# Loading the value product's repeated weight block with its other six tiles, and preparing the fourth pair's right block one product sooner

## The chip, the cores and the metric

The kernel runs on one core of a Trainium2 chip. The metric is the device time of one execution in microseconds (us). The engines are TensorE (PE; its weight loads are listed as PEld), VectorE (DVE), ScalarE (ACT), GpSimd (POOL) and SyncE (SP), which here issues all DMAs.

## The reference

One layer of a streaming encoder, with 1024 positions of width 1024, in fp32. Two attentions run side by side, of 8 heads of 64 each: one over a band of 9 chunks of 64 positions with a learned bias, and one of the stick-breaking kind.

```python
def reference(x, w_in, b_gate, rel_bias, w_proj_a, w_proj_b, w_out,
              ln1_g, ln1_b, w_ffn_in, w_ffn_out, ln2_g, ln2_b):
    ...
        h = x @ w_in[l]
        qa, ka, va, qb, kb, vb, ga, gb = jnp.split(h, split_pts, axis=-1)
        ...
        y_a = chunk_band_attention(heads_a(qa), heads_a(ka), heads_a(va), rel_bias[l]) @ w_proj_a[l]
        y_b = stick_breaking_attention(heads_b(qb), heads_b(kb), heads_b(vb)) @ w_proj_b[l]
        gate_a = jax.nn.sigmoid(ga + b_gate[l, :D])
        gate_b = jax.nn.sigmoid(gb + b_gate[l, D:])
        mix = (gate_a * y_a + gate_b * y_b) @ w_out[l]
        x = layer_norm(DEEPNORM_ALPHA * x + mix, ln1_g[l], ln1_b[l])
        gu = x @ w_ffn_in[l]
        g, u = jnp.split(gu, 2, axis=-1)
        ffn = (jax.nn.silu(g) * u) @ w_ffn_out[l]
        x = layer_norm(DEEPNORM_ALPHA * x + ffn, ln2_g[l], ln2_b[l])
    return x
```

The change lies in the first product, `x @ w_in`.

## The kernel before

**How a product is made.** Every operand is split into a high part (rounded, by a cast on ScalarE) and a low part (what is left, by a subtraction on VectorE); the helper `split` does both, at lines 110 and 111. Each product of two operands is three matmuls: high by high, high by low, low by high. On top of that the kernel multiplies block matrices of 2 x 2 blocks with seven products instead of eight. The seven are called p1 to p7 and run in the order 1, 2, 6, 5, 7, 3, 4. Some of them need sums or differences of blocks as their weights, and VectorE makes those: for a pair called `p3`, `tap3` and `tbp3` are such differences (lines 151, 152, 153 and 159, of the raw left block `wLp3` and right block `wRp3`). `wbp3h` and `wbp3l` are the high and low part of `tbp3`, `wap3h` and `wap3l` those of `tap3`, and `wcp3` holds both parts for p3.

**The order of the work.** `work` is a list: four pairs of q and k columns (tiles p0 to p3), the fifth q and k pair (p4), then the value columns V of all heads (at index `V_AT`, 5), then the other q and k pairs, then the gates. `run_pairs` emits the seven steps of each in turn. The left block of a pair (`left`, line 129) and its right block (`right`, which calls `prep_right` at line 140 and `prep_last` at line 162) are emitted between the steps of the pairs ahead. For the first three lists of steps, p1 and p2 are emitted ahead of everything (`first=3`). At the end of each pair, line 388 (ScalarE) and line 389 (VectorE) scale and split q and k, and lines 335 and 336 store them (`q_dr`, `k_dr`).

**The value product.** Here the weights are the moving operand's blocks, and its accumulators are four banks (`v1_0` to `v1_3` for p1, used again by p6; `v2_0` to `v2_3` for p2). `v_load` asks for six raw tiles, the halves of blocks 0, 2 and 3 of V's weights: `wv0_0`, `wv0_1`, `wv2_0`, ... . `v_prepare` makes the operands of one product from them. Block 1 is needed in differences for p6 (lines 434, 435 and 436) and for p7 (line 438), and is loaded for each of them at line 432, as `wv1_60` and `wv1_61` for p6. The differences are written over the tiles that they read. The high and low parts are `vh6_0`, `vl6_0` (first half), `vh6_1`, `vl6_1`. Line 479 issues the matmuls, line 489 (ScalarE) and 491 (VectorE) take the results out of the banks into tiles `vc11_0` and so on, and line 459 stores them to `v_dr`.

**Who decides the order.** The program order above is where each instruction is written. A scheduler then places the instructions of each engine, except a few that are kept as written. Buffers come from rotating pools with fixed numbers (`gt` 3, `kp` 4, `op` 8): a new tile waits until the last reader of the tile that had its buffer is done. `cycle(QKV, ...)` takes buffers in turn from four pools that the attention uses later. SyncE issues all DMAs in one queue, in order.

Of the kernel before, what the change touches and what calls it, by code (L numbers as in the profile page):

```python
# [48 lines left out]
def hybrid_trunk_kernel(ctx: ExitStack, tc, x, xt, w_first, w_v, w_in, b_gate, rel_bias, w_proj,  # L49
# [14 lines left out]
    def slot(tag, name, dtype=F32):  # L64
        return pool.tile([P, 1024], dtype, tag=tag, name=name, bufs=SLOTS[tag])
# [3 lines left out]
    def cycle(tags, name, dtype=F32):  # L69

        turn_of[tags] = turn_of.get(tags, -1) + 1
        return slot(tags[turn_of[tags] % len(tags)], name, dtype)

    QKV = ("qs", "kh", "kl", "v")
# [9 lines left out]
    dma = nc.sync.dma_start  # L84
# [24 lines left out]
    def split(dst_h, dst_l, src):  # L109
        return (nc.scalar.copy(dst_h, src),  # L110
                nc.vector.tensor_tensor(dst_l, src, dst_h.bitcast(F32), ALU.subtract))  # L111
# [28 lines left out]
    def prep_right(W, nm, src, tag, tag_a=None):  # L140
        W["R"] = slot("gt", f"wR{nm}")
        dma(W["R"], src)
        right_sums_b(W, nm, tag)
        right_sums_a(W, nm, tag_a or tag)
# [17 lines left out]
    def prep_last(W, nm, tag):  # L162

        c = slot(tag, f"wc{nm}", F32R)
        split(c[:, LO], c[:, HI], W["R"][:, HI])
        W["c"] = c
# [69 lines left out]
    V_AT = 5  # L236
# [6 lines left out]
    def left(i):  # L243
        prep_left(Wa[i], f"p{i}", w_in[work[i][2]])

    def right(i):
        prep_right(Wa[i], f"p{i}", w_in[work[i][3]], "op")
        prep_last(Wa[i], f"p{i}", "kp")
# [161 lines left out]
    v_src = [[None] * 2 for _ in range(3)]  # L410
    v_ops = {}

    def v_load():

        for n, (blk, tags) in enumerate(((0, ("gt", "gt")), (3, ("gt", "kp")), (2, ("kp", "kp")))):
            for h, tag in enumerate(tags):
                v_src[n][h] = slot(tag, f"wv{blk}_{h}")
        for n, blk in ((0, 0), (2, 2), (1, 3)):
            for h in range(2):
                dma(v_src[n][h], w_v[blk, h])  # L420

    def v_prepare(p):

        put, sub = nc.vector.tensor_tensor, ALU.subtract
        v_ops[p] = []
        for h in range(2):
            X, U, Z = (v_src[n][h] for n in range(3))
            hi, lo = (slot("op", f"v{s}{p}_{h}", F32R) for s in "hl")
            src = {1: X, 2: Z, 5: X, 3: U, 4: Z}.get(p)
            if src is None:  # L430
                src = cycle(QKV, f"wv1_{p}{h}") if p == 6 else slot("gt", f"wv1_{p}{h}")
                dma(src, w_v[1, h])
                if p == 6:
                    put(X, src, X, sub)
                    put(src, U, X, sub)
                    put(Z, Z, src, sub)
                else:
                    put(src, U, src, sub)
            split(hi, lo, src)
            v_ops[p].append((hi, lo))  # L440

    def v_steps():
# [18 lines left out]
        def step(p, following):  # L461
# [3 lines left out]
            def run():  # L465
                if following:
                    v_prepare(following)
                if first:
                    for j in range(4):
                        tag = ("mm", "mm", "sc", "sc")[j] if accs is by else ("tr", "tr", "tr", "pv")[j]  # L470
                        accs[j] = bank(tag, f"v{p}_{j}")
                for h in range(2):
                    for j in range(4):
                        for i in range(2):
                            kt = 2 * h + i
                            xh_, xl_ = (x[:, j * P:(j + 1) * P] for x in ops_x[p][kt])
                            wh, wl = (w[:, (LO, HI)[i]] for w in v_ops[p][h])
                            for n, (a, b) in enumerate(((xh_, wh), (xh_, wl), (xl_, wh))):
                                mm(accs[j], a, b, start=(first and kt == n == 0),  # L479
                                   stop=(kt == 3 and n == 2), skip_group_check=True)  # L480
                for j in range(4):
                    acc = spread(accs[j])
                    if p == 4:
                        done("21", j, acc)
                        continue
                    name = {1: "11", 2: "11", 6: "12", 3: "12", 5: "22", 7: "22"}[p]
                    raw = tile_of(name, j)[1]
                    if p in (1, 6, 5):
                        nc.scalar.copy(raw, acc)
                    else:  # L490
                        nc.vector.tensor_tensor(raw, acc, raw, ALU.add)
                        done(name, j, raw)
# [9 lines left out]
            store_proj(i - len(work) + 9)  # L502

    def run_pairs(steps, left, right, also=lambda i: None, first=2, aside=lambda i: None,
                  then=lambda: None, wide=None):

        n = len(steps)
        for j in range(first):
            steps[j][0]()
            steps[j][1]()  # L510
        then()
        for i in range(n):
            rest = steps[i][2:] if i < first else steps[i]
            for j, p in enumerate(rest):
                p()
                if i == wide:
                    if j == 5:
                        left(i + 1)
                    if j == 6:
                        right(i + 1)  # L520
                        left(i + 2)
                    continue
                if j == 0 and i + 1 < n:
                    right(i + 1)
                if j == 1 and i + 2 < n and wide not in (i + 1, i + 2):
                    left(i + 2)
                aside(i)
            also(i)
# [74 lines left out]
    def left_again(i):  # L603
        Wa[i]["L"] = slot("gt", f"wLp{i}")
        dma(Wa[i]["L"], w_in[work[i][2]])
# [21 lines left out]
    def right_or_v(i):  # L627
        if i + 1 == V_AT:
            v_load()
            v_prepare(1)  # L630
        else:
            right(i + 1)

    run_pairs([v_steps() if i == V_AT else project(i) for i in range(1, len(work))],
              lambda i: left(i + 1) if i > 2 else left_again(3) if i == 2 else None,
              right_or_v, first=3, then=rest_of_start, also=aside_work, wide=V_AT - 1)
    first_gate = 2 * N_GATE
    first_w = begin_gate(first_gate, nc.vector)()

# [611 lines left out]
    def second_half():  # L1251
# [3 lines left out]
    plain_half(LO, ops_1[1] + ops_1[2], second_half)  # L1255
    prep_last(Wf[1], "f1", "op")
    run_pairs([up_steps(f) for f in range(1, NF)], lambda i: left_f(i + 1) if i > 1 else None,
              lambda i: right_f(i + 1), first=2, aside=next_piece, then=plain_rest)

# [3 lines left out]
    def load_plain(f0, f1, tags):  # L1263
        hs = []
        take = lambda name, dtype: cycle(tags, name, dtype)
        for f in range(f0, f1):
            hs.append(load_w(h_dr[f], f"h{f}", of("gt"), take, nc.vector) +
                      load_w(w_ffn_out[f * P:(f + 1) * P, :], f"fo{f}", of("gt"), take,
                             nc.vector))
        return hs  # L1270
# [88 lines left out]
    first = load_plain(0, 2, ("bw", "bw", "kp", "kp", "bw", "bw", "bw", "kp"))  # L1359
# [67 lines left out]
```

## Time and profile before

| what | value |
|---|---|
| runs | 1443.1, 1443.45, 1443.83 us (median 1443.45) |
| profiled execution | 1444.35 us, span 1442.6 us |
| PE busy | 1421.1 us (99%), 6696 matmuls |
| VectorE, ScalarE, GpSimd busy | 1028.6, 673.0, 267.8 us |
| granted TensorE clock | 0.994 mean |

The profile is of one execution. Its rows give a start in us from the start of the span, then a duration, the engine, the line of the kernel, the operation and the tiles (buffer numbers left out), the shape, and how many were merged (x12). In square brackets stands the idle time of the engine before the row and what ended it. A granted clock of 1.00 is TensorE at full speed.

### The profile page before, as it was taken

How to read it: one execution, taken by the hardware profiler on the slowest of the kernel's cores; microseconds unless marked ns; L12 is line 12 of the kernel's file. 1: busy time of each engine (PE TensorE's matmuls, PEld its weight loads, DVE VectorE, ACT ScalarE, POOL GpSimd, SP SyncE). 2: the span in 40 equal slices, each digit the busy share in tenths (PEclk: the TensorE clock that was granted, in tenths of full speed). 3: DMA queues.
4: the chain of work that ended last, by engine and by line, in shares of the span. 5: the costliest groups of instructions: out<-in, count | busy, mean ns of one | idle time of the engine just before them, and what ended most of it. 6: DMA issues, size and time to landing. Idle time of an engine off the chain costs nothing.

```text
span 1442.6 us, 19078 instructions
## 1 busy us (share of the span) xinstructions
PE 1421.1 (99%) x6696; PEld 1178.6 (82%) x6696; DVE 1028.6 (71%) x1638; ACT 673.0 (47%) x1171; POOL 267.8 (19%) x317
## 2 busy tenths in 40 slices
PE   9997999999999999999999999999999999999997
PEld 7785888888888888888888888888888888888886
DVE  8856565654777878887858966676777755978757
ACT  6443444555787888773313634444444433221201
POOL 0000000001555778850014000000000000100016
PEclk9998999999999999999999999999999999999999
DMA  7565357868677587867512123434444457786602
GB/s 248 149 203 165 127 205 220 283 205 251 195 214 193 166 239 239 270 197 274 178 37 95 55 106 127 143 143 157 161 160 146 150 201 260 287 306 240 204 15 103
DMA packets 102544, 263.99 MB, mean 183 GB/s; under 512 B 11040, under 2 KB 27424, under 8 KB 102448
## 3 DMA queue, kind: packets, MB, share of 16 engines
q1 hardware_dynamic: 102448, 262.77, 55.5%
q8 instruction: 53, 0.87, 0.3%
q14 instruction: 43, 0.35, 0.1%
HBM read 170.94 MB, written 88.11 MB: 180 GB/s over the span
## 4 chain that ended last, share of the span: by engine, by line
PE 93%; DVE 3%; ACT 1%; DMA 1%; issue 1%; POOL 0%; SPq 0%; POOLq 0%; DVEq 0%; ACTq 0%
PE sxf L180 16%; PE sxp L180 8%; PE szf L180 8%; PE dx L1350 6%; PE v L479 5%; PE gps L573 4%; PE szp L180 4%; PE syf L180 4%; PE dz L1350 3%; PE yAps L870 3%; PE syp L180 2%; PE tp_b L781 2%; PE tp_a L781 2%; PE ops L118 2%; PE ops L117 2%; PE ops L120 2%
## 5 line engine op out<-in xcount | busy, mean ns | idle before, releaser
L1306 POOL TENSOR_TENSOR wdyt<-wdyt 128x512 f32<-128x512 f32 x8 | 11.1, 1394 | 512.3 <-ACT h L1178 422.6
L758 POOL TENSOR_TENSOR w_b<-w_b,kp_b 128x511 f32<-128x511 f32 (+3 forms) x96 | 96.4, 1015 | 31.8 <-DVE kp_b L753 22.5
L753 DVE TENSOR_TENSOR_SCAN kp_b<-kp_b,ident_ps 128x512 f32<-128x512 f32 (+2 forms) x64 | 56.6, 885 | 23.3 <-ACT kp_b L750 22.4
L750 ACT ACTIVATE kp_b<-sc_b 128x512 f32<-128x512 f32 (+3 forms) x96 | 48.4, 504 | 30.7 <-PE sc_b L670 25.4
L1058 POOL TENSOR_TENSOR mv<-mv,neghalf 128x1 f32<-128x1 f32 x16 | 23.9, 1494 | 207.6 <-DVE mv L1057 207.6
L693 POOL MEMSET bias<- 64x64 f32 x2 | 0.3, 145 | 327.3 <-ACT bias L689 327.3
L180 PE MATMUL szf<-x1S63h,wcf 128*128 128x512 f32 x168 | 55.1, 389 | 0.0
L111 DVE TENSOR_TENSOR pt_b<-tp_b,pt_b 128x512 fp32r<-128x512 f32 (+1 forms) x96 | 50.0, 544 | 6.8 <-ACT pt_b L110 6.2
L1281 DVE TENSOR_TENSOR x<-dx,x 128x512 f32<-128x512 f32 x64 | 43.5, 687 | 14.9 <-PE dx L1350 14.9
L723 POOL TENSOR_SCALAR w_a<-w_a,st_a 128x640 f32<-128x640 f32 (+2 forms) x64 | 42.4, 667 | 61.6 <-PE sc_a L670 26.5
L111 DVE TENSOR_TENSOR sl<-h,sl 128x512 fp32r<-128x512 f32 x56 | 38.5, 687 | 20.1 <-ACT sl L110 20.1
L110 ACT CAST sl<-h 128x512 fp32r<-128x512 f32 x56 | 34.7, 619 | 36.2 <-PE syf L180 17.1
L110 ACT CAST pt_b<-tp_b 128x512 fp32r<-128x512 f32 (+1 forms) x96 | 47.5, 505 | 8.0 <-PE tp_b L781 7.6
L718 ACT ACTIVATE w_a<-w_a,st_a 128x640 f32<-128x640 f32 (+2 forms) x64 | 44.8, 700 | 12.4 <-DVE st_a L712 11.2
L118 PE MATMUL ops<-wl_o,mh 128*128 128x512 f32 x128 | 50.1, 392 | 0.0
L120 PE MATMUL ops<-wh_o,ml 128*128 128x512 f32 x128 | 49.9, 390 | 0.0
L117 PE MATMUL ops<-wh_o,mh 128*128 128x512 f32 x128 | 49.7, 391 | 0.0
L1178 ACT ACTIVATE h<-sxf 128x512 f32<-128x512 f32 x21 | 12.6, 598 | 77.7 <-PE sxf L180 77.7
L751 ACT ACTIVATE w_b<-sc_b 128x511 f32<-128x511 f32 (+3 forms) x96 | 48.6, 506 | 0.0
L781 PE MATMUL tp_b<-ident,w_b 128*128 128x128 f32 x288 | 47.8, 273 | 0.4 <-DVE pt_b L111 0.3
L111 DVE TENSOR_TENSOR pt_a<-tp_a,pt_a 128x512 fp32r<-128x512 f32 (+1 forms) x96 | 44.8, 485 | 4.6 <-ACT pt_a L110 3.1
L110 ACT CAST pt_a<-tp_a 128x512 fp32r<-128x512 f32 (+1 forms) x96 | 39.1, 432 | 11.0 <-PE tp_a L781 10.7
(1740 smaller groups left out, 4784.8 us busy)
## 6 DMA issues: line engine op xcount, KB each, us to landing
s_dr<-sl SPq DMA_DIRECT2D x112, 256.0 KB, 2.3
sd<-s_dr SPq DMA_DIRECT2D x56, 512.0 KB, 4.8
wLf<-in_w_ffn_in_dram SPq DMA_DIRECT2D x22, 512.0 KB, 4.5
wRf<-in_w_ffn_in_dram SPq DMA_DIRECT2D x22, 512.0 KB, 3.5
v_dr<-vc SPq DMA_DIRECT2D x16, 512.0 KB, 3.0
kh<-k_dr SPq DMA_DIRECT2D x32, 256.0 KB, 5.8
kl<-k_dr SPq DMA_DIRECT2D x32, 256.0 KB, 6.0
qs<-q_dr SPq DMA_DIRECT2D x16, 512.0 KB, 5.5
```

Of the source, the lines that this page charges most:

```text
L110: return (nc.scalar.copy(dst_h, src), nc.vector.tensor_tensor(dst_l, src, dst_h.bitcast(F32), ALU.subtract))
L111: nc.vector.tensor_tensor(dst_l, src, dst_h.bitcast(F32), ALU.subtract))
L117: mm(acc, lh, rh, start=(i == 0), stop=False)
L118: mm(acc, lh, rl, start=False, stop=False)
L120: mm(acc, ll, rh, start=False, stop=(i == n))
L180: mm(acc, lw[:, ks], rx, start=(first and kt == i == 0), stop=(kt == 3 and i == 2), skip_group_check=not first)
L479: mm(accs[j], a, b, start=(first and kt == n == 0), stop=(kt == 3 and n == 2), skip_group_check=True)
L573: mm(acc[hf], lw[:, ks], rx[k][:, (LO, HI)[hf]], start=(k == j == 0), stop=(k == KT - 1 and j == 2))
L753: nc.vector.tensor_tensor_scan(kp[:, 0:e], kp[:, 0:e], ident_ps()[:, 0:e], 0.0, ALU.mult, ALU.add)
L758: nc.gpsimd.tensor_tensor(be[:, m0:e], be[:, m0:e], kp[:, m0 - 1:e - 1], ALU.mult)
L781: tr(tp[:, (qb - lo_q) * P:(qb - lo_q + 1) * P], wt[qb - q0][:, (kb - qb) * P:(kb - qb + 1) * P], ident)
L1350: mm(acc, a, b, start=(first and i == n == 0), stop=(i == n - 1 == 1), skip_group_check=not first)
```

## The change

`v_load` takes two more buffers, `wv1_60` from the pool `kp` and `wv1_61` from the cycle, and loads block 1 into them directly after the other six tiles. `v_prepare` for p6 uses these tiles and loads nothing; for p7 it loads as before. `run_pairs` has a new argument, `then_right=2`: the right block of the fourth pair (p3) is emitted after p7 of the second pair (p1), and no longer after p6 of the third (p2). In between lay p3 and p4 of the second pair and p6 of the third. The call of `run_pairs` for the FFN does not pass the argument.

```diff
--- before.py
+++ after.py
@@ -415,26 +415,30 @@
         for n, (blk, tags) in enumerate(((0, ("gt", "gt")), (3, ("gt", "kp")), (2, ("kp", "kp")))):
             for h, tag in enumerate(tags):
                 v_src[n][h] = slot(tag, f"wv{blk}_{h}")
+        again = [slot("kp", "wv1_60"), cycle(QKV, "wv1_61")]
         for n, blk in ((0, 0), (2, 2), (1, 3)):
             for h in range(2):
                 dma(v_src[n][h], w_v[blk, h])
+        for h in range(2):
+            dma(again[h], w_v[1, h])
+        v_src.append(again)
 
     def v_prepare(p):
 
         put, sub = nc.vector.tensor_tensor, ALU.subtract
         v_ops[p] = []
         for h in range(2):
-            X, U, Z = (v_src[n][h] for n in range(3))
+            X, U, Z, Y = (v_src[n][h] for n in range(4))
             hi, lo = (slot("op", f"v{s}{p}_{h}", F32R) for s in "hl")
             src = {1: X, 2: Z, 5: X, 3: U, 4: Z}.get(p)
             if src is None:
-                src = cycle(QKV, f"wv1_{p}{h}") if p == 6 else slot("gt", f"wv1_{p}{h}")
-                dma(src, w_v[1, h])
+                src = Y if p == 6 else slot("gt", f"wv1_{p}{h}")
                 if p == 6:
                     put(X, src, X, sub)
                     put(src, U, X, sub)
                     put(Z, Z, src, sub)
                 else:
+                    dma(src, w_v[1, h])
                     put(src, U, src, sub)
             split(hi, lo, src)
             v_ops[p].append((hi, lo))
@@ -502,7 +506,7 @@
             store_proj(i - len(work) + 9)
 
     def run_pairs(steps, left, right, also=lambda i: None, first=2, aside=lambda i: None,
-                  then=lambda: None, wide=None):
+                  then=lambda: None, wide=None, then_right=None):
 
         n = len(steps)
         for j in range(first):
@@ -520,8 +524,10 @@
                         right(i + 1)
                         left(i + 2)
                     continue
-                if j == 0 and i + 1 < n:
+                if j == 0 and i + 1 < n and i + 1 != then_right:
                     right(i + 1)
+                if j == 2 and i + 2 == then_right:
+                    right(i + 2)
                 if j == 1 and i + 2 < n and wide not in (i + 1, i + 2):
                     left(i + 2)
                 aside(i)
@@ -633,7 +639,7 @@
 
     run_pairs([v_steps() if i == V_AT else project(i) for i in range(1, len(work))],
               lambda i: left(i + 1) if i > 2 else left_again(3) if i == 2 else None,
-              right_or_v, first=3, then=rest_of_start, also=aside_work, wide=V_AT - 1)
+              right_or_v, first=3, then=rest_of_start, also=aside_work, wide=V_AT - 1, then_right=2)
     first_gate = 2 * N_GATE
     first_w = begin_gate(first_gate, nc.vector)()
```

The number of instructions of each engine stays the same; their order changes from the second pair to the value product, and at the start of the attention. Lines of the changed kernel after 418 are shifted: 434, 435, 436 are now 437, 438, 439, line 459 is 463, and line 491 is 495.

The first place is VectorE (DVE), behind the low parts of the third pair's right block (the right block of p3 is `wRp3`, its left block `wLp3`; `c1_1` and `c2_1` are q and k of the second pair). Before:

```order
L195 TENSOR_TENSOR c2_1_643<-szp1_664,c2_1_643 128x512
L151 TENSOR_TENSOR tap3_749<-wRp3_747,wLp3_678 128x512
L159 TENSOR_TENSOR tap3_749<-wRp3_747 128x512
L152 TENSOR_TENSOR tbp3_750<-wRp3_747,tap3_749 128x512
L389 SCALAR_TENSOR_TENSOR c2_1_643<-c2_1_643,hi2_1_706 128x1024
L389 SCALAR_TENSOR_TENSOR c1_1_533<-c1_1_533,hi1_1_726 128x1024
L153 TENSOR_TENSOR tbp3_750<-wLp3_678,tbp3_750 128x512
L111 TENSOR_TENSOR wcp3_763<-wRp3_747,wcp3_763 128x512
L111 TENSOR_TENSOR wbp3l_755<-tbp3_750,wbp3h_754 128x1024
L111 TENSOR_TENSOR wap3l_760<-tap3_749,wap3h_759 128x1024
```

The same stretch of VectorE now:

```order
L151 TENSOR_TENSOR tap3_695<-wRp3_693,wLp3_678 128x512
L159 TENSOR_TENSOR tap3_695<-wRp3_693 128x512
L152 TENSOR_TENSOR tbp3_696<-wRp3_693,tap3_695 128x512
L195 TENSOR_TENSOR c2_1_643<-szp1_664,c2_1_643 128x512
L153 TENSOR_TENSOR tbp3_696<-wLp3_678,tbp3_696 128x512
L111 TENSOR_TENSOR wcp3_709<-wRp3_693,wcp3_709 128x512
L389 SCALAR_TENSOR_TENSOR c1_1_533<-c1_1_533,hi1_1_745 128x1024
L111 TENSOR_TENSOR wbp3l_701<-tbp3_696,wbp3h_700 128x1024
L111 TENSOR_TENSOR wap3l_706<-tap3_695,wap3h_705 128x1024
L389 SCALAR_TENSOR_TENSOR c2_1_643<-c2_1_643,hi2_1_725 128x1024
```

The three subtractions (lines 151, 152, 153) and line 159 now stand ahead of both steps of line 389, and that of `c2_1` comes last.

The second place is SyncE around V's weights (`rel_dr` is the table of the bias, `k_dr4` and `q_dr4` are k and q of the fifth pair). Before, the stretch that ends with the two loads of line 432 (the six loads lie further up):

```order
L335 DMA q_dr4_81<-hi1_4_1069 64x1024
L336 DMA q_dr4_81<-c1_4_959 64x1024
L335 DMA q_dr4_81<-hi1_4_1069 64x1024
L336 DMA q_dr4_81<-c1_4_959 64x1024
L432 DMA wv1_61_1155<-in_w_v_dram 128x1024
L459 DMA v_dr0_93<-vc11_0_1136 128x1024
L432 DMA wv1_60_1146<-in_w_v_dram 128x1024
```

The stretch of SyncE with these two loads (now line 423) now:

```order
L329 DMA rel_dr_213<-rel_sb_939 8x896
L421 DMA wv3_0_963<-in_w_v_dram 128x1024
L421 DMA wv3_1_964<-in_w_v_dram 128x1024
L423 DMA wv1_60_967<-in_w_v_dram 128x1024
L423 DMA wv1_61_968<-in_w_v_dram 128x1024
L335 DMA k_dr4_89<-hi2_4_1053 64x1024
L336 DMA k_dr4_89<-c2_4_1011 64x1024
L335 DMA k_dr4_89<-hi2_4_1053 64x1024
L336 DMA k_dr4_89<-c2_4_1011 64x1024
```

Before, `wv1_61` and `wv1_60` were issued behind the stores of the fifth pair's q, one of them behind the first store of V; now both stand ahead of the fifth pair's k as well.

The third place is VectorE in the value product (`c1_4` is q of the fifth pair, `v2_0` a bank of V's p2). Before:

```order
L389 SCALAR_TENSOR_TENSOR c1_4_959<-c1_4_959,hi1_4_1069 128x1024
L491 TENSOR_TENSOR vc11_0_1136<-v2_0_1162,vc11_0_1136 128x8x64
L491 TENSOR_TENSOR vc11_1_1138<-v2_1_1163,vc11_1_1138 128x8x64
L111 TENSOR_TENSOR vc11_0_1136<-vc11_0_1136 128x8x64
L491 TENSOR_TENSOR vc11_2_1140<-v2_2_1164,vc11_2_1140 128x8x64
L111 TENSOR_TENSOR vc11_1_1138<-vc11_1_1138 128x8x64
L491 TENSOR_TENSOR vc11_3_1142<-v2_3_1165,vc11_3_1142 128x8x64
L111 TENSOR_TENSOR vc11_2_1140<-vc11_2_1140 128x8x64
L111 TENSOR_TENSOR vc11_3_1142<-vc11_3_1142 128x8x64
L434 TENSOR_TENSOR wv0_1_962<-wv1_61_1155,wv0_1_962 128x1024
L435 TENSOR_TENSOR wv1_61_1155<-wv3_1_964,wv0_1_962 128x1024
L436 TENSOR_TENSOR wv2_1_966<-wv2_1_966,wv1_61_1155 128x1024
```

VectorE behind the same line 389 now:

```order
L389 SCALAR_TENSOR_TENSOR c1_4_959<-c1_4_959,hi1_4_1073 128x1024
L437 TENSOR_TENSOR wv0_0_961<-wv1_60_967,wv0_0_961 128x1024
L438 TENSOR_TENSOR wv1_60_967<-wv3_0_963,wv0_0_961 128x1024
L437 TENSOR_TENSOR wv0_1_962<-wv1_61_968,wv0_1_962 128x1024
L439 TENSOR_TENSOR wv2_0_965<-wv2_0_965,wv1_60_967 128x1024
L111 TENSOR_TENSOR vl6_0_1149<-wv1_60_967,vh6_0_1148 128x1024
L438 TENSOR_TENSOR wv1_61_968<-wv3_1_964,wv0_1_962 128x1024
L495 TENSOR_TENSOR vc11_0_1140<-v2_0_1162,vc11_0_1140 128x8x64
L439 TENSOR_TENSOR wv2_1_966<-wv2_1_966,wv1_61_968 128x1024
L111 TENSOR_TENSOR vl6_1_1156<-wv1_61_968,vh6_1_1155 128x1024
L111 TENSOR_TENSOR vc11_0_1140<-vc11_0_1140 128x8x64
L495 TENSOR_TENSOR vc11_1_1142<-v2_1_1163,vc11_1_1142 128x8x64
```

The differences of p6 (434 to 436 before, 437 to 439 now) come directly behind line 389, and the results of p2 are taken out of their banks between and behind them.

## The prediction

> **What bounds the kernel now.** I read the page first, for the share of each engine.
>
> ```profile
> span 1442.6 us, 19078 instructions
> PE 1421.1 (99%) x6696; PEld 1178.6 (82%) x6696; DVE 1028.6 (71%) x1638; ACT 673.0 (47%) x1171; POOL 267.8 (19%) x317
> ```
>
> PE is the bound nearly everywhere. The diff leaves the number of matmuls alone, so it can gain only what PE waits, or runs slowly, in the stretch it touches. Next came the waits of PE (engine, line, what it waited for; total us, times, longest).
>
> ```profile
> PE v L479 <- ACT vh L110: 9.3, 1, 9.3
> ...
> PE sxp L180 <- ACT wbp3h L110: 0.4, 1, 0.4
> ```
>
> One long wait stands out: a product of V (line 479) waits for `vh`, the high part of its weights. A short one names `wbp3h`, the fourth pair's right block (its tile p3). Those are the two things that the diff prepares differently. Third, the timeline of PE at the short one, and the steady pace from a run of 12 matmuls without a wait.
>
> ```profile
> 63.31 0.39 PE L180 MATMUL szp<-s13h,wap2l 128*128 128x512 f32 x1
> 64.11 0.50 PE L180 MATMUL sxp<-s24h,wbp3h 128*128 128x512 f32 x1 [0.41 <-ACT wbp3h L110]
> ...
> 65.70 0.39 PE L180 MATMUL sxp<-s24h,wbp3h 128*128 128x512 f32 x1
> 341.70 2.72 PE szp L180 x12
> ```
>
> The last row, a piece of the chain of waits, gives 2.72 / 12 = 0.227 us a matmul. From 63.31 to 65.70 are five steps (counted in the timeline): 2.39 us where 5 x 0.227 = 1.13 would do. **Stall A is 1.26 us**, not the 0.41 that the one wait shows. Fourth, the same for the long wait, and the windows around it (columns: window and length, busy of PE, PEld, DVE, ACT, POOL, then granted clock, DMA share, GB/s).
>
> ```profile
> 127.71 0.39 PE L479 MATMUL v<-vh,xl 128*128 128x512 f32 x1
> 137.38 1.65 PE L479 MATMUL v<-vh,s24h 128*128 128x512 f32 x3 [9.28 <-ACT vh L110]
> ...
> 143.66 0.39 PE L479 MATMUL v<-vh,s24h 128*128 128x512 f32 x1
> 127.70:137.40 9.70, 0.42 (x3) 0.02 (x1) 9.41 (x10) 2.15 (x4) 0.00 (x0) 0.77 0.77 264
> 137.40:143.20 5.80, 5.80 (x14) 4.34 (x15) 4.65 (x5) 2.77 (x3) 0.00 (x0) 0.50 0.21 56
> ```
>
> PE stands from 127.71 + 0.23 = 127.94 to 137.38, 9.44 us, and comes back at a granted clock of 0.50, which lasts 5.80 us. The matmul at 143.66 is the 16th after that at 127.71 (counted in the timeline): 15.95 us where 16 x 0.227 = 3.63 would do. **Stall B is 12.32 us**: 9.44 of waiting and 2.88 of slow clock.
>
> **Why stall A is there, and what the change does to it.** VectorE and ScalarE in front of it:
>
> ```profile
> 57.61 0.69 DVE L195 TENSOR_TENSOR c<-szp,c 128x512 f32<-128x512 f32 x1
> 58.21 0.69 DVE L151 TENSOR_TENSOR tap<-wRp,wLp 128x512 f32<-128x512 f32 x1
> ...
> 60.01 2.36 DVE L389 SCALAR_TENSOR_TENSOR c<-c,hi 128x1024 f32<-128x1024 f32 x2
> 62.28 0.69 DVE L153 TENSOR_TENSOR tbp<-wLp,tbp 128x512 f32<-128x512 f32 x1
> 60.69 0.61 ACT L110 CAST wcp<-wRp 128x512 fp32r<-128x512 f32 x1
> 63.01 1.05 ACT L110 CAST wbp3h<-tbp 128x1024 fp32r<-128x1024 f32 x1 [1.71 <-DVE tbp L153]
> ```
>
> No load is late: line 151 reads `wRp3` at 58.21 without a wait. What is late is the last subtraction (line 153), because two steps of an older pair (line 389, 2.36 us) stand before it. In the changed order of VectorE the three subtractions come before line 195 and all of line 389: from 57.61 on that is L151, L159, L152, L195, L153, at the rows' pace of 0.60 us each, so L153 starts at 57.61 + 4 x 0.60 = 60.0 and not at 62.28, 2.3 us earlier. If the load allowed L151 only at 58.21, it would be 1.7. ScalarE is busy with what stands ahead of the cast until 60.69 + 0.61 = 61.3, so I take 1.7 us for `wbp3h`, the lower value; the stall needs 64.11 - 63.54 = 0.57 at its first step and 1.26 in all, so 0.4 is to spare. `wap3h`, cast right behind, moves with it. **Gain 1.26 us**; if the cover were gone it would be 0, and below nothing only if line 389, now last, were missed: it feeds stores of k and q, which nobody reads until the attention heads after 340 us. The load `wRp3` is issued where it was.
>
> **Why stall B is there.** SyncE's queue, VectorE and ScalarE:
>
> ```profile
> 102.63 1.56 SPq L420 DMA_DIRECT2D wv<-in_w_v_dram  x2
> ...
> 121.04 1.01 SPq L432 DMA_DIRECT2D wv<-in_w_v_dram  x1
> 126.73 0.33 SPq L459 DMA_DIRECT2D v_dr<-vc  x1
> 127.18 0.37 SPq L432 DMA_DIRECT2D wv<-in_w_v_dram  x1
> DMA to landing us min/median/max: 3.5/4.6/5.7
> 117.92 1.22 DVE L389 SCALAR_TENSOR_TENSOR c<-c,hi 128x1024 f32<-128x1024 f32 x1
> 133.77 1.23 DVE wv L434
> 135.03 1.24 DVE wv L435
> 136.28 1.05 ACT vh L110
> ```
>
> The two repeated weight tiles (line 432) are issued at 121.04 and 127.18; the second stands in SyncE's queue behind a store of V that goes out at 126.73. It lands some 4.6 us later (the row of V's weight tiles), and only then can the second line 434 run, at 133.77; line 435 and ScalarE's cast follow, and PE starts at 137.38, which is 3.61 us after that line 434.
>
> In the changed kernel both loads follow the six others in SyncE's queue, with nothing of V's stores ahead. The six end with 102.63 + 1.56 = 104.2. The first of the two has to wait until its buffer is free: it was the third-product weights (`wcp4`), whose last matmul moves 22 places later:
>
> ```profile
> 98.25 0.39 PE L180 MATMUL szp<-s24h,wcp 128*128 128x512 f32 x1
> 117.60 1.06 ACT L489 COPY vc<-v 128x512 f32<-128x512 f32 x2
> 124.06 0.69 DVE L491 TENSOR_TENSOR vc<-v,vc 128x512 f32<-128x512 f32 x1 [4.92 <-PE v L479]
> ```
>
> 98.25 + 0.39 + 22 x 0.227 = 103.6, less the 1.26 gained: 102.4, so that wait costs SyncE nothing. Issued by about 104 to 105, both land by 105 + 5.7 = 111. VectorE then reaches the subtractions when line 389 is done: 117.92 + 1.22 - 1.26 = 117.9. Its new steps there take 1.23 us each (as at 133.77): the first half's 434 and 435, done 120.4, then ScalarE's cast of 1.05, so `vh` of the first half at 121.4. PE, 1.26 us earlier, wants it at 127.94 - 1.26 = 126.7: **5.3 us to spare**. The second half is ready on VectorE after four steps more (125.3), cast 126.3, its low part after three more, one of 0.60, at 128.4; PE wants it 18 matmuls into the product, at 126.7 + 18 x 0.227 = 130.8, so 2.4 us to spare. The tightest is the bank of the fourth column: ScalarE's copy out of it (line 489 before, 0.53 us, half of the row at 117.60) now comes behind the cast of the third column, which needs VectorE's steps of lines 111 and 491 behind 128.4 (three of 0.60): 130.2, the cast (0.61, as at 60.69) and the copy, 131.3; wanted at 126.7 + 24 x 0.227 = 132.1. That leaves 0.8 us. **Gain 12.32 us**, the slow clock included, as PE no longer stands. What is late next is nothing that I can find up to the seventh product, whose reload is issued behind V's stores as before.
>
> Moved past on SyncE: the two loads now precede the eight stores of `k_dr4` and `q_dr4`; these were first issued at 113 in the trace, 8 us after the loads are out. Each load holds its buffer some 20 us longer; it is free again once the cast's low part is out (about 124 and 128), before the next pair's right block asks for one.
>
> [...]
>
> **The sum.** The profiled execution took 1444.35 us, 1.75 more than its span. 1444.35 - 1.26 - 12.32 = 1430.77. The median of the runs, 1443.45, is 0.90 below the profiled one: **1429.9 us**.
>
> **The rivals.**
>
> *A residue stays in V's second product* (chance 0.12). The last bank has 0.8 us to spare and the second half 2.4; what speaks for it is that VectorE's row from 117.9 to 130.2 has no gap, so each microsecond late at its start (line 389 waits for ScalarE) arrives at PE but for that. One step of 1.23 us late costs 0.4, three cost 2.9: **1430.3 to 1432.8**. Against it: before, VectorE had 4.92 us idle ahead of 124.06. [...]
>
> *The start of the attention pays* (0.08). The changed order moves loads of head 1 on SyncE: `kl1` goes from before the stores of the gates to behind them and behind `v1`.
>
> ```profile
> 347.79 2.92 DMA g_dr<-c
> 350.73 4.52 DMA v<-v_dr
> 355.27 0.44 PE L781 MATMUL tp_a<-ident,w_a 128*128 128x128 f32 x2 [0.19 <-DMA v<-v_dr]
> kl<-k_dr SPq DMA_DIRECT2D x32, 256.0 KB, 6.0
> ```
>
> Issued when that store has landed (350.7), `kl1` is there at 350.7 + 6.0 = 356.7; head 1's scores ran from about 355.5 before and stand some 10 matmuls later in the new row of PE (357.9). Missing it by one place in the queue (a load of 4.5 us) costs 3.3: **1431 to 1433.2**. For it: PE already waited there, 0.19 us.
>
> *Only stall B goes* (0.04): 1429.9 + 1.26 = **1431.2**. *Only stall A goes* (0.03), the change not doing what it says because the loads still land late: 1443.45 - 1.26 = **1442.2**, within what can be measured.
>
> *Slower* (0.05). SyncE issues in order, and the first of the two loads waits there for its buffer; all eight stores of k and q and V's stores stand behind it. PE loses nothing if line 434 starts by 126.7 - 3.6 = 123.1, so if the load is issued by 123.1 - 5.7 = 117.4. The whole gain is gone when PE waits 10.7 us and then 2.88 at half clock, that is from an issue at 128.1: a hold of 24 us after 104. Then each microsecond costs one, and a hold of 28 us gives **1447**. The reader that I found frees it at 102.4; only a reader that I missed could do this.
>
> **How the numbers follow.** The forecast (both stalls go, at most 0.5 us left) has 0.68. Faster are it and the rivals but two: 0.68 + 0.12 + 0.08 + 0.04 = 0.92; only A is within 0.2% (2.9 us, about what a measurement of this kernel can tell from no change): 0.03; slower 0.05. The range: 1434.0 takes in both kinds of residue, with 0.8 for the spread of the runs; 1428.5 is the forecast less that spread (0.7) and less 0.7 for short waits, such as the 0.19 at line 781, that a new order may also lose. Beyond it are only A and slower, 0.08, and a little on both sides.
>
> **What would show it.** In the changed profile: no PE wait for `wbp3h` and 12 matmuls in 2.72 us around 62; both repeated loads issued by about 105 in the list of SyncE's issues; no idle time of PE near 126.7; a clock of 1.00 in the windows up to 143; PE busy lower by about 3 us (matmuls at half clock are longer) and the span lower by 13.6. It is wrong if PE waits over 1 us for `vh`, for a V bank or for `kl`, or if the loads are issued after 117.

## The result, and the profile after

| | median | runs | ratio to before |
|---|---|---|---|
| before | 1443.53 us | 1443.10 to 1443.83 (4) | |
| changed | 1431.28 us | 1430.44, 1430.51, 1432.06, 1435.49 | 0.9921 [0.9901, 0.9941] |

The change makes the kernel faster by 12.3 us, 0.8%. The profiled execution took 1430.51 us with a span of 1428.7, where the prediction's sum, made against the profiled one of before, said 1430.77. Two further measurements of the same kernel, below, gave medians of 1430.74 and 1430.57; over all twelve runs the median is 1430.6, with four runs of 1432 and more.

First the waits of TensorE in the changed kernel (columns as before):

```profile
PE warm L267 <- DVE warm L264: 1.2, 1, 1.2
PE tp_a L787 <- DVE pt_a L111: 0.4, 1, 0.4
PE tp_b L787 <- DVE pt_b L111: 0.3, 1, 0.3
```

The wait of 9.3 us for `vh` and that of 0.4 for `wbp3h` are gone, and no new one stands in their place. Second, the timeline of TensorE at the two places, and the windows around the second.

```profile
62.84 0.39 PE L180 MATMUL szp<-s13h,wap2l 128*128 128x512 f32 x1
63.06 0.39 PE L180 MATMUL sxp<-s24h,wbp3h 128*128 128x512 f32 x1
63.29 0.39 PE L180 MATMUL sxp<-s24l,wbp3h 128*128 128x512 f32 x1
63.73 0.50 PE L180 MATMUL sxp<-s24h,wbp3l 128*128 128x512 f32 x1
64.07 0.39 PE L180 MATMUL sxp<-s24h,wbp3h 128*128 128x512 f32 x1
64.30 0.39 PE L180 MATMUL sxp<-s24l,wbp3h 128*128 128x512 f32 x1
...
126.06 0.39 PE L483 MATMUL v<-vh,xl 128*128 128x512 f32 x1
126.29 0.39 PE L483 MATMUL v<-vh,s24h 128*128 128x512 f32 x1
126.52 0.39 PE L483 MATMUL v<-vl,s24h 128*128 128x512 f32 x1
...
126.00:132.00 6.00, 6.00 (x28) 4.95 (x28) 6.00 (x10) 3.56 (x7) 0.00 (x0) 1.00 0.29 115
132.00:138.00 6.00, 6.00 (x28) 4.99 (x27) 1.78 (x2) 2.85 (x5) 0.00 (x0) 1.00 0.95 337
138.00:144.00 6.00, 6.00 (x29) 4.95 (x28) 5.13 (x5) 3.16 (x3) 0.00 (x0) 1.00 0.33 95
```

V's second product follows the first at the steady pace, 126.06 to 126.29, at a clock of 1.00. At the fourth pair the five steps from 62.84 to 64.30 take 1.46 us, where they took 2.39 and 1.13 would do: 0.33 us is left there, around the first matmul with the low part `wbp3l`, at 63.73. Third, the queue of SyncE and the steps of VectorE and ScalarE that carried the prediction's bounds:

```profile
101.01 1.62 SPq L421 DMA_DIRECT2D wv<-in_w_v_dram  x2
102.72 0.85 SPq L423 DMA_DIRECT2D wv<-in_w_v_dram  x2
...
117.33 1.22 DVE L437 TENSOR_TENSOR wv<-wv,wv 128x1024 f32<-128x1024 f32 x1
118.58 1.23 DVE L438 TENSOR_TENSOR wv<-wv,wv 128x1024 f32<-128x1024 f32 x1
119.84 1.05 ACT L110 CAST vh<-wv 128x1024 fp32r<-128x1024 f32 x1 [3.22 <-DVE wv L438]
126.00 1.22 DVE L111 TENSOR_TENSOR vl<-wv,vh 128x1024 fp32r<-128x1024 f32 x1
130.46 0.57 ACT L493 COPY vc<-v 128x512 f32<-128x512 f32 x1
```

The repeated tiles are out by 103.6. `vh` of the first half is ready at 120.9 for a product that wants it at 126.3, which leaves 5.4 us. The second half's low part is ready at 127.2, 3.4 us ahead of its first use, and the copy out of the fourth bank ends at 131.0, wanted 24 matmuls after 126.29, at 131.7: 0.7 us to spare.

### The profile page after: what moved, and what is told of

It reads as the page before. It is cut to its first block, busy times and chain, and to the rows that moved or that the text cites. A ratio compares the mean times of both kernels' runs of the same rounds, so it can differ in the third digit from the quotient of the medians.

```text
span 1428.7 us, 19071 instructions
## 1 busy us (share of the span) xinstructions
PE 1417.4 (99%) x6696; PEld 1177.0 (82%) x6696; DVE 1027.6 (72%) x1638; ACT 672.7 (47%) x1171; POOL 267.8 (19%) x317
## 4 chain that ended last, share of the span: by engine, by line
PE 94%; DVE 3%; ACT 1%; DMA 1%; POOL 0%; issue 0%; POOLq 0%; SPq 0%; DVEq 0%; ACTq 0%
PE sxf L180 16%; PE sxp L180 8%; PE szf L180 8%; PE dx L1356 6%; PE v L483 5%; PE gps L579 4%; PE syf L180 4%; PE szp L180 4%; PE dz L1356 3%; PE yAps L876 3%; PE syp L180 2%; PE tp_b L787 2%; PE tp_a L787 2%; PE ops L118 2%; PE ops L117 2%; PE ops L120 2%
## 5 line engine op out<-in xcount | busy, mean ns | idle before, releaser
L1184 ACT ACTIVATE h<-sxf 128x512 f32<-128x512 f32 x21 | 12.5, 598 | 77.9 <-PE sxf L180 77.9
```

## The experiments

**Each edit alone.** The first kernel moves only the right block:

```diff
+                if j == 2 and i + 2 == then_right:
+                    right(i + 2)
 ...
-    ... also=aside_work, wide=V_AT - 1)
+    ... also=aside_work, wide=V_AT - 1, then_right=2)
```

> The right block moved, V's loads as before. Theory (two separate stalls): stall A goes, of 1.26 us some 0.9 to 1.3, so 1442.2 to 1442.6 against 1443.5; PE still waits about 9.4 us for vh in V's second product and runs at half clock behind it. Rival (the right block also helps V, since everything ahead of V is earlier): over 3 us gained, 1440 or less. Rival (the move only shifts VectorE's work and another PE wait takes its place): 1443.5, with a new PE wait near 60 to 70 us.

Measured: 1442.92 us (11 runs, 1441.6 to 1445.5), before 1443.38, ratio 0.9996 [0.9988, 1.0005]. In its profile the wait for `wbp3h` is gone, as the theory has it, but the time can't be told from before, and the interval (1.7 us gained to 0.7 lost) doesn't exclude the forecast gain of 0.9 to 1.3 either. The profile shows two more things, behind the wait in V and much later:

```profile
135.82 1.65 PE L479 MATMUL v<-vh,s24h 128*128 128x512 f32 x3 [9.29 <-ACT vh L110]
...
138.58 0.46 PE L479 MATMUL v<-vl,s24h 128*128 128x512 f32 x1
138.88 0.40 PE L479 MATMUL v<-vh,s24l 128*128 128x512 f32 x1
...
573.32 0.47 PE L672 MATMUL sc_b<-kl,qs 128*128 128x512 f32 x1 [1.29 <-DMA kl<-k_dr]
```

The wait for `vh` is as long as before and simply begins and ends 1.6 us earlier (its end at 135.82, not 137.38), but matmuls are back at the full pace after about 2.9 us, not 5.8. And in the stick-breaking attention PE waits 1.29 us for head 13's `kl`. So in that execution 2.9 us are gained at the attention's first score (344.05 against 346.98); 0.3 of it was there before the change's first instruction, and 1.4 is the shorter slow stretch, counted to the 16th matmul. Between the first and the last score 1.8 us are lost again, 1.29 of them in the wait for `kl`.

The second kernel has only V's loads moved (`then_right=2` left out):

```diff
-    ... also=aside_work, wide=V_AT - 1, then_right=2)
+    ... also=aside_work, wide=V_AT - 1)
```

> V's two loads early, the right block as before. Theory: stall B goes whole, 12.3 us, so 1431.2; stall A stays with 0.41 us before wbp3h. Rival (the loads alone leave a residue, since without the earlier right block PE and VectorE meet differently in V): a PE wait of 1 us or more for vh or a bank of V, 1432 to 1434.

Measured: 1432.06 us (5 runs, 1431.84 to 1432.48), ratio 0.9920 [0.9906, 0.9933], 0.9 above the 1431.2 expected. No wait for `vh`, and the 0.41 before `wbp3h` stands as it did. Its profile's first score comes 12.5 us earlier than before, 0.2 of which was there at 41 us already: 12.3, the size of stall B; 0.6 of it is lost again by the end (span 1430.7 against 1442.6). The changed kernel, on the same chip:

> The changed kernel once more, since its first four runs spread from 1430.4 to 1435.5 where those of before spread by 0.7 us. Theory (disturbance from outside, rare): nearly all runs at 1430.5 within 0.5. Rival (a wait with little cover, such as the copy out of V's fourth bank with 0.7 us or head 1's kl load, that is missed in some runs): again one run in two to four 1.5 to 5 us longer, at a granted clock lower by 0.001 to 0.002, while the loads-only and right-only kernels tell by their own spread which of the two edits brings it.

Measured: 1430.74 us (1430.40, 1430.46, 1431.01, 1432.05). So, between the medians, the right block is worth 1.3 us on top of the loads; one of its four runs, 1432.05, lies among those of loads only. Its profiled execution, the one of 1431.01, holds a short form of the same late wait:

```profile
561.09 0.47 PE L676 MATMUL sc_b<-kl,qs 128*128 128x512 f32 x1 [0.32 <-DMA kl<-k_dr]
```

**Place or buffer?** The change alters both where the loads are written and which buffer the first gets. Two kernels separate them. Before, with the buffer of the change:

```diff
-                src = cycle(QKV, f"wv1_{p}{h}") if p == 6 else ...
+                src = (slot("kp", f"wv1_{p}{h}") if h == 0 else cycle(QKV, f"wv1_{p}{h}")) if p == 6 else ...
```

> The kernel before, with one thing altered: the first of the two repeated tiles (wv1_60) takes its buffer from the pool kp, as in the change, but is still loaded where line 432 stands. It asks whether the buffer or the place in the program made the load late. Theory (the place: the load is written behind the stores of the fifth pair's k and q, and VectorE takes p2's results out before it subtracts): wv1_60 goes out at about 121 again, its line 434 runs only behind the four results of p2, at about 130, so vh at about 133.6 and a wait of 5 to 6 us, with half the gain or less: 1437 to 1440. Rival (the buffer): wv1_60 goes out by 116, and the stall is gone or under 3 us: 1434 or less.

Measured: 1440.67 us (10 runs, 1439.7 to 1441.7), ratio 0.9982 [0.9972, 0.9991].

```profile
120.24 1.04 SPq L432 DMA_DIRECT2D wv<-in_w_v_dram  x1
129.33 1.22 DVE L434 TENSOR_TENSOR wv<-wv,wv 128x1024 f32<-128x1024 f32 x1
132.94 1.65 PE L479 MATMUL v<-vh,s24h 128*128 128x512 f32 x3 [5.63 <-ACT vh L110]
```

The load goes out at 120.24 all the same, and line 434 runs behind p2's four results: the wait shrinks to 5.63 us, inside the 5 to 6 of the place theory, because the half that PE wants first is now also loaded first. The time is 0.7 above its range: in V it saves 4.2 us (its first score of the attention comes 5.0 us earlier, at 342.0 and not 347.0, of which 0.8 was there ahead of V), but at the end of the span 3.1 of the 5.0 are left, and the profile lists small later waits of 0.3 to 0.4 us that before does not have. And the loads-only kernel with both tiles from the cycle, as before has them (asked for earlier, they need not be the same buffers of it):

```diff
-        again = [slot("kp", "wv1_60"), cycle(QKV, "wv1_61")]
+        again = [cycle(QKV, "wv1_60"), cycle(QKV, "wv1_61")]
```

> The loads-only kernel, with both repeated tiles in buffers of the cycle (as before), loaded early with the other six. Theory (the place): stall B goes whole, as with loads only: 1432.0 within 0.5, no wait of PE for vh over 0.5 us. Rival (the buffer): the loads wait in SyncE's queue for stores of q and k out of those buffers, stand out after 110, and hold the queue: a PE wait of 2 us or more, 1434 or more.

Measured: 1432.40 us (4 runs, 1432.1 to 1432.8), ratio 0.9924 [0.9908, 0.9940], as loads only, and its list of waits has none for `vh`. So the place in the program brings 10.9 to 11.3 us with either choice of buffers, and the buffer alone, at the old place, 2.6. Written early, the loads also bring the subtractions ahead of p2's results on VectorE; no kernel here has one of these without the other, so how much belongs to each is not shown.

**The half clock.** Stall B was summed as 9.44 us of waiting and 2.88 of slow clock. Useless matmuls in the wait are to take away the second without the first:

```diff
+                if p == 6:
+                    fill = bank("mm", "fill")
+                    for n in range(36):
+                        mm(fill, xh[0][:, 0:P], xh[1][:, LO], start=(n == 0), stop=(n == 35))
```

> The kernel before, with 36 matmuls of no use (8.2 us at 0.227) put between V's first and second product's wait, into a free bank, so that TensorE works while it would wait; the loads stay late. It separates the two parts of stall B. Theory (2.88 us of the 12.32 are the half clock that follows the wait): the wait of 9.44 stays as filling plus about 1.2 us of idle time, the clock stays at 1.00, and the time is 1443.5 - 2.9 = 1440.6. [...] Rival (the slow matmuls behind the wait come from late operands, not from the clock): 1443.5.

> The filled wait with 24 matmuls in place of 36: the filling ends 2.7 us earlier, so TensorE stands about 3.9 us and not 1.1 before V's second product. It asks how long a wait must be to bring the half clock. [...] Theory from the trace of before (9.44 us bring it, 0.4 do not): open between the two; with a half clock behind the wait it is 1443.4, as before.

Measured with 36: 1441.60 us, ratio 0.9988 [0.9979, 0.9996], so 1.8 us gained (0.6 to 3.0); with 24: 1443.89, ratio 1.0003 [0.9993, 1.0013], nothing gained. First the rows with 36, then those with 24:

```profile
127.11 0.39 PE L483 MATMUL v<-vh,xl 128*128 128x512 f32 x1
127.34 8.32 PE L475 MATMUL fill<-xh,xh 128*128 128x512 f32 x36
136.79 1.21 PE L483 MATMUL v<-vh,s24h 128*128 128x512 f32 x4 [1.13 <-ACT vh L110]
...
140.73 0.39 PE L483 MATMUL v<-vh,s24l 128*128 128x512 f32 x1
137.40:143.20 5.80, 5.70 (x25) 4.40 (x24) 4.06 (x4) 2.19 (x3) 0.00 (x0) 1.00 0.33 87
```

```profile
127.40 5.60 PE L475 MATMUL fill<-xh,xh 128*128 128x512 f32 x24
136.85 1.65 PE L483 MATMUL v<-vh,s24h 128*128 128x512 f32 x3 [3.85 <-ACT vh L110]
134.00:138.00 4.00, 1.15 (x3) 0.83 (x3) 3.93 (x4) 2.25 (x3) 0.00 (x0) 0.74 0.15 62
137.40:143.20 5.80, 5.80 (x16) 4.30 (x15) 4.12 (x4) 2.24 (x3) 0.00 (x0) 0.54 0.31 83
```

With an idle time of 1.13 us the clock stays at 1.00, and the 16th matmul after V's first product comes 13.62 us after its last (127.11 to 140.73; counted in the timeline), not 15.95: 2.33 us less. With 3.85 us idle, in the profiled execution, the half clock is there as after 9.28, and the same distance is 15.96 (127.17 to 143.13). So the slow clock is a cost of its own, and a wait of 3.85 us can bring it; what lies between 1.13 and 3.85 us these two kernels do not show. With 24, the clock fell 2.9 us after the end of the last useless matmul (133.0 to 135.9; a clock of 0.74 over the 4 us up to 138.0 is 2.1 us of half clock). The interval of the gain in the times with 36 (0.6 to 3.0 us) takes in both the 2.33 seen in place and the 2.88 of the sum.

**How much cover the new chain has.** Useless steps on VectorE ahead of the cast of `vh`, in the changed kernel, six and three of them:

```diff
                     put(src, U, X, sub)
+                    for _ in range(6 if h == 0 else 0):
+                        put(src, src, src, ALU.max)
```

> The changed kernel, with six steps of no use (the maximum of a tile with itself, 1.2 us each) put on VectorE between line 438 of the first half and the cast of vh. It asks whether the cover that the prediction counted (5.3 us for vh) is there. Theory: the first half of vh is ready at about 132.8 instead of 120.9, PE wants it at 126.3, so a PE wait of about 6.5 us for vh, and a half clock behind it of up to 2.9 us: 1430.7 + 6.5 + 0 to 2.9 = 1437.2 to 1440.1, up to 1 more for the low part behind it. Rival (the cover is larger, or PE takes other work first): under 1434.

> The changed kernel with three steps of no use (1.2 us each) between line 438 of the first half and the cast of vh, where six made PE wait 6.5 us. Theory (a short wait costs only itself, as the filled wait of 1.1 us showed): vh at about 127.6 where PE wants it at 126.3, a wait of about 1.3 us for vh, perhaps 0.5 more for the low part, clock 1.00: 1432 to 1432.7. Rival (any wait on this place brings the half clock): 1434 or more. Rival (no wait at all, the cover being larger than counted): 1430.7.

Measured with six: 1441.78 us (10 runs, 1439.6 to 1443.1), ratio 0.9989 [0.9979, 0.9998]; with three: 1435.09 (5 runs, 1434.6 to 1436.2), ratio 0.9942 [0.9930, 0.9955]. First the rows with six, then those with three:

```profile
132.99 2.07 PE L485 MATMUL v<-vh,s24h 128*128 128x512 f32 x4 [6.51 <-ACT vh L110]
133.00:138.00 5.00, 5.00 (x12) 3.69 (x13) 5.00 (x6) 3.33 (x5) 0.00 (x0) 0.50 0.26 105
```

```profile
128.54 0.96 PE L485 MATMUL v<-vh,s24h 128*128 128x512 f32 x3 [1.30 <-ACT vh L110]
130.34 0.50 PE L485 MATMUL v<-vl,s24h 128*128 128x512 f32 x1 [0.83 <-DVE vl L111]
130.00:134.00 4.00, 3.66 (x16) 3.04 (x17) 4.00 (x7) 2.73 (x5) 0.00 (x0) 1.00 0.28 113
```

The waits for `vh` are 6.51 and 1.30 us, as counted (6.5 and 1.3). With six the half clock follows; with three it does not, so the expectation's rival, a half clock after any wait, is out, although the time of 1435.09 lies in its range. Both times came out longer than said, by 0.7 and 2.4 us. With six, V's second product pays 9.3 us (its 16th matmul at 139.03 stands 12.94 behind the first product's last, at 126.09), which is inside the 6.5 to 9.4 expected; the profiled run loses some 1.4 us more than the changed kernel from the attention on. With three, I had counted the low part behind `vh` too lightly (0.83 us of wait of its own). In that profile V's second product pays 2.7 us (its 16th matmul at 133.20 stands 6.35 us behind the first product's last, at 126.85, where it took 3.63); another 0.8 was there ahead of V's second product (126.85 against 126.06) and 0.7 came in the attention, and why stays open.

**The spread of the runs.** Head 13's `kl` is issued behind the store of `m_dr0`, in a stretch where the DMA share is 1.04 (550 to 555 us, in the changed kernel's profile and the repeated one). Asked for earlier, it goes out ahead of that store:

```diff
-        if hidx < 14 and pos == 8:
+        if hidx < 14 and pos == (8 if hidx < 8 else 6):
             load_qk(heads[hidx + 2])
```

> The changed kernel, with q and k of the stick-breaking heads' second next head asked for two steps earlier in the attention loop (position 6 instead of 8). In SyncE's order that puts head 13's kl ahead of the store of m_dr0 and of the load of gA2 and moves little else. In the right-only and the repeated run PE waited 1.29 and 0.32 us for this load, which came 9 to 10 us after its issue; in the first run of the changed kernel it came after 7.2 us and nothing waited. Theory (this load's landing is what spreads the runs): no PE wait on kl, the load issued 4 us earlier, and all runs at 1430.4 to 1430.8. Rival (the spread has other causes): runs of 1431 to 1435 remain, at a lower granted clock.

> The changed kernel a third time, beside the one with the earlier kl of head 13 on the same chip, so that the two can be told apart by less than one us. Theory: median 1430.7, some runs up to 1432; the other kernel 0 to 0.5 us shorter. Rival (the earlier load pushes the loads that it overtakes): the other kernel is longer.

Measured: 1430.37 us (1429.78, 1430.25, 1430.50, 1430.58) with the earlier load, 1430.57 (1430.09, 1430.52, 1430.63, 1432.50) without. First the issue with the earlier load, then without:

```profile
544.21 1.25 SPq L659 DMA_DIRECT2D kl<-k_dr  x2
```

```profile
551.69 1.28 SPq L659 DMA_DIRECT2D kl<-k_dr  x2
```

The load is out 7.5 us earlier and takes longer, 10.2 us to its landing, so that it is there 5.5 us earlier. No wait on `kl` is left in its profile, but there was none in this profile of the other either. The medians can't be told apart. All four runs with the earlier load are short, but so are eight of the twelve without it, so four don't show that the spread is gone. The stretch without it, in three profiled executions (rows of `kl`'s landing around its issue: changed, repeated, right only), and the DMA share in the repeated one (1.04, columns as before):

```profile
DMA to landing us min/median/max: 6.5/6.9/7.2
```

```profile
DMA to landing us min/median/max: 7.6/8.3/9.0
550.00:555.00 5.00, 5.00 (x32) 4.33 (x31) 3.83 (x8) 3.56 (x9) 5.00 (x12) 1.00 1.04 343
```

```profile
DMA to landing us min/median/max: 8.8/9.4/10.0
```

The load takes 7.2, 9.0 and 10.0 us in its later half, and PE's wait goes with it: none, 0.32 and 1.29 us. So this load's landing costs 0.3 to 1.3 us in two profiled executions. Why it takes longer in some is not shown: the first one, where it took 7.2, has the same share of 1.04 in this window. What made the run of 1435.49 stays open.

## Why the prediction was right

**Stall B, 12.32 us.** This step held in place: between the last matmul of V's first product and the 16th behind it lie 3.63 us now and lay 15.95 before. Loads only brings the same 12.3 us by the start of the attention. The bounds were about there: 5.4 us to spare for `vh` (said: 5.3) and 0.7 for the fourth bank (said: 0.8). The split into waiting and slow clock held as well: filling the wait brought 1.00 in the clock row and 2.33 of the 2.88 us (with the wait filled, TensorE loses 0.4 us ahead of the first low part, at 138.11). One reading did not hold: in the trace of before, line 434 of the first half did not wait for the second load to land. First the landing of that load, issued at 127.18, counted from its issue, then VectorE:

```profile
DMA to landing us min/median/max: 4.9/4.9/4.9
...
130.12 1.22 DVE L434 TENSOR_TENSOR wv<-wv,wv 128x1024 f32<-128x1024 f32 x1
131.37 1.23 DVE L435 TENSOR_TENSOR wv<-wv,wv 128x1024 f32<-128x1024 f32 x1
132.63 1.22 DVE L436 TENSOR_TENSOR wv<-wv,wv 128x1024 f32<-128x1024 f32 x1
133.77 1.22 DVE L434 TENSOR_TENSOR wv<-wv,wv 128x1024 f32<-128x1024 f32 x1
```

The load was there at 132.1. VectorE came to this line only at 133.77, straight from the other half's three steps, and its list shows no idle time since 125.42. So in the trace of before it was VectorE's order, p2's results and the other half first, that held `vh` last. The size of the stall, read at TensorE, does not depend on this reading, and the change moves both the load and VectorE's steps.

**Stall A, 1.26 us.** The mechanism was right, the term a little large: 0.93 of the 1.26 went at these steps. The prediction followed `wbp3h` and `wap3h` and left the low part out, and it called line 389 "now last" where only one of its two steps is; the other, that of `c1_1`, stands ahead of `wbp3l` on VectorE:

```profile
61.32 1.22 DVE L389 SCALAR_TENSOR_TENSOR c<-c,hi 128x1024 f32<-128x1024 f32 x1
62.45 1.22 DVE L111 TENSOR_TENSOR wbp3l<-tbp,wbp3h 128x1024 fp32r<-128x1024 f32 x1
```

The cast of `wbp3h` is done at 62.24, so this order costs `wbp3l` about 0.2 us of the 0.33 that are left; where the rest comes from is not shown. Up to V's second product the changed kernel gains 1.2 us in the traces (127.71 against 126.06, less 0.47 that were there from the start); in the medians the edit is worth 1.3 us beside the loads. Alone it shows no gain that can be measured (0.9996); in its trace the wait in V does not take up the gain but moves earlier with it, and most of it goes again in the attention.

**The median.** 1431.28 is 1.4 above the 1429.9 forecast, the profiled execution 0.3 below its own sum. The step behind it is the last one, the 0.90 that I took off to get from the profiled execution to the median: before, the profiled run was at the long end of the runs, now it is at the short end. That the sum and the profiled execution agree to 0.3 is partly luck: 0.47 us were there from the start (the last matmul ahead of the fourth pair's product stands at 62.84, not 63.31), 0.33 of stall A stayed, and 0.25 more went between the two stalls, where the prediction has no term.

**The rivals.** By the number alone, 1431.28 lies in the range of both residues, in V and at the start of the attention; the traces speak against them. V's second product keeps its pace (3.63 us to the 16th matmul). The start of the attention, where `kl1` was moved, shows no wait of TensorE. The place in the attention that does cost something in some executions is head 13, which the prediction did not look at. The rival of a queue held on SyncE falls: the two loads are out 0.9 us after the six (103.6 against 102.6).

## What to carry to other kernels

A wait can cost more than its length. Here TensorE's waits of 3.85 to 9.29 us in V's second product cost their length and a slow clock as well, those of 1.13 and 1.30 us no slow clock, and in the changed kernel wait and slow clock are both gone: sum the two from the matmul before the wait to the first one that is back at pace. When a load is late, ask whether its buffer or its place in the program holds it, and look at what the consuming engine does ahead of it: here the right half first, at the old place, gained 2.6 us; written early, so that its subtractions too came ahead of other work, 11.3. Look in the trace as well as at the time for what a small edit does alone: here the small stall went and the large wait behind it came earlier by as much, and the measured time still could not show it.

## What the runs showed of the hardware

The half clock came with idle times of 3.85 (24 matmuls), 5.63 (`wv1_60` from `kp`), 6.51 (six steps), 9.28 (before) and 9.29 us (right only), and not with 1.13 (36 matmuls) or 1.30 (three steps). Its length does not follow the wait: TensorE worked at half clock for about 2.9 us in the right-only kernel and 5.8 in the kernel before, after the same wait of 9.3. It began within the wait, so part of it fell on idle time. Two windows of right only:

```profile
127.70:137.40 9.70, 1.58 (x4) 1.10 (x5) 9.47 (x10) 2.89 (x4) 0.00 (x0) 0.72 0.57 212
137.40:143.20 5.80, 5.80 (x24) 4.71 (x24) 3.21 (x4) 1.21 (x2) 0.00 (x0) 0.89 0.42 134
```

A mean of 0.72 over 9.70 us is 5.4 us at half clock, and 0.89 over 5.80 another 1.3: 6.7 us. In the kernel before, 0.77 over 9.70 and 0.50 over 5.80 give 10.3. In windows of 0.2 us the clock of before is 0.50 from 133.0 to 143.2, 10.2 us, and 1.00 on both sides. From its two means, the half clock of right only lasted from about 132.0 to 138.7 if it was one stretch. Three other traces have it, by windows of 4 us for 6.8 to 6.9 us each: 24 matmuls (0.74, 0.50, 0.91 from 134.0 on), `wv1_60` from `kp` (0.59, 0.55 from 130.0 on) and six steps (0.68, 0.50, 0.97 from 130.0 on). Why it lasted longer in the trace of before than in these four is not shown. What the wait of 9.3 us cost in slow clock by the 16th matmul differs with it: 1.5 us in the right-only trace, 2.88 in that of before. One load of head 13's k landed 7.2 to 10.0 us after its issue in three executions of the same stretch, and with it TensorE's wait went from none to 1.29 us.
